# Seven products in the last feed-forward stage, rows to tokens by SP's queue, sides of x from scaled tiles

## The chip, the cores and the metric

The kernel runs as one program on one core of one Trainium2 chip. The time is that of the device from start to end, in microseconds; the kernel before took 956.64 us, the median of three runs (956.61 to 957.17). Lower is better.

## The reference

Two decoder layers work on 256 tokens of 1024 features (x, kept in float32). Each layer has four sublayers that add to x: a feed-forward stage, a token mixer (layer 0: a short gated convolution beside sliding-window attention; layer 1: block attention), cross-attention to a memory of 256 rows, and a second feed-forward stage. A final normalization ends it. The change works inside the feed-forward stages:

```python
def rmsnorm(x, g):
    x32 = x.astype(jnp.float32)
    y = x32 * lax.rsqrt(jnp.mean(x32 * x32, axis=-1, keepdims=True) + EPS)
    return y.astype(x.dtype) * g

def swiglu(x, w_gate, w_up, w_down):
    return (jax.nn.silu(x @ w_gate) * (x @ w_up)) @ w_down

for l in range(DEPTH):
    x = x + 0.5 * swiglu(rmsnorm(x, ffn1_norm[l]), ffn1_w_gate[l], ffn1_w_up[l], ffn1_w_down[l])
    ...
    x = x + 0.5 * swiglu(rmsnorm(x, ffn2_norm[l]), ffn2_w_gate[l], ffn2_w_up[l], ffn2_w_down[l])
return rmsnorm(x, final_norm)
```

w_gate and w_up are 1024 x 2816, w_down is 2816 x 1024. There are four such stages: ffn1 of layer 0, ffn2 of layer 0, ffn1 of layer 1 and ffn2 of layer 1, which is the last work before the final normalization.

## The kernel before

**x and its splits.** x lies with its features on the 128 partitions: eight tiles `x[:, k]` of 128 features by 256 tokens. Every product keeps float32's accuracy by splitting both factors into a rounded high part and the rest: x·w is taken as high·high + high·low + low·high, three matmuls for one. The scale of a norm is a number per token and is multiplied in when a product leaves PSUM, so a stage's matmuls start on x times the norm's gain.

**The stream of weights.** All weights come in one stream (class `Stream`) in chunks of 16 tiles of 128 x 128, 1 MB each. SP issues the loads into four buffers `raw` (`_load_to`); a load waits until VectorE (DVE) and ScalarE (ACT) are done with the buffer's last content. A chunk is two blocks of eight tiles. For each block ACT writes the high part `whi` (L143) and DVE the low part `wlo` (L144), into five buffers each, so that the splits run up to four blocks ahead of TensorE (PE).

**The order of the work.** `Order` is a planner that emits the instructions: a list of fillers (pieces of matmuls, each with a planned cost) and tasks put in with `pe.after(delay, fn, cost)`, which are emitted when the planner's clock, in planned ns, has come to their time. Afterwards a scheduler may still move an instruction along its engine's queue, except one marked `keep_in_program_order`, which stays behind all that its engine had been given before.

**A feed-forward stage** (`ffn`). The hidden width of 2816 is worked through in five groups of four tiles (512 columns) and one of two. For a group, `rows_of` computes gate and then up with tokens on the partitions: per tile of x (eight), half of the tokens (two) and part of the split (three) a matmul of 128 x 512, so 2 · 8 · 2 · 3 = 96 matmuls for a group. They are emitted in pieces (`part`) of 12 matmuls, which use one block of weights. The product of silu(gate) and up is turned back to features on partitions by `turned_back`: two DVE transposes, a store to DRAM and four loads on POOL's queue, and 22 to 34 us later (planned) a split by ACT and DVE into `h`. When gate and up are done, the down products follow: `downs` with features on partitions, and in the last stage `down_tok` with tokens on partitions, since the result leaves in that order.

**Seven products for eight** (`seven`, SEVEN = 12: the fourth group). Two of the four stages, named in `AT` with their place in the stream, compute this one group by a scheme of the Strassen kind. The factors are cut in four: x by halves of the tokens and halves of the features, the weights by halves of the features and by gate | up. Eight products of quarters would be 96 matmuls; seven products of sums of quarters are 7 · 4 · 3 = 84. Each is a filler of 12 matmuls that uses two blocks. `PLACES` says between which pieces of the other groups they stand. The sums of weight quarters are made by DMA: `load_bases` and `add` issue seven transfers of 1 MB on POOL's queue, five of which add to a tile in place of overwriting it; two further chunks come through SP's stream. The sums of x's quarters, the "sides", are made by DVE and ACT: `side` and `side2`, four times each, one for each pair of feature tiles (k, k + 4).

**The last stage's other work.** `to_tokens` brings x into token order for the final sum: four DVE transposes, and for each of them eight stores of 32 KB (in rows of 32 numbers) on POOL's queue to a DRAM tile `tok`, then one load of 1 MB into `xtok` on the same queue. `gfin`, the final gain, is loaded by SP to all partitions. `evac_tok` adds the down products to `xtok`, multiplies by the gain and the norm's factor, and stores the output.

Of the kernel before, what the change touches and what calls it, by code (L numbers as in the profile page):

```python
# [15 lines left out]
F32 = mybir.dt.float32  # L16
F32R = mybir.dt.float32r
AF = mybir.ActivationFunctionType
ALU = mybir.AluOpType
# [4 lines left out]
P = 128  # L24
# [24 lines left out]
AT = {("ffn2", 0): 52, ("ffn1", 1): 88}  # L49
# [216 lines left out]
def build(nc, tc, ctx, a):  # L266
# [50 lines left out]
    def col(key, k):  # L317
        c = VCOL[key] + k
        return vecs[:, c:c + 1]
# [188 lines left out]
    def to_tokens(out):  # L508


        tok = dram.tile([S, D], F32, name="tok")
        to = tok.rearrange("(c i) (k p j) -> p k i c j", i=32, p=4, j=32)
        for k in range(0, KT, 2):
            t = act.tile([P, 2 * S], F32, name="q2", bufs=2)
            tc.keep_in_program_order(nc.vector.transpose(t, x[:, k:k + 2].rearrange("p k s -> p (k s)")))
            for p in range(4):
                for i in range(2):
                    tc.keep_in_program_order(nc.gpsimd.dma_start(
                        to[p, k + i], t[32 * p:32 * p + 32, i * S:(i + 1) * S].rearrange("i (c j) -> i c j", j=32)))
        nc.gpsimd.dma_start(out, tok.rearrange("(u q) f -> q u f", u=2))  # L520
# [20 lines left out]
    def ffn(which, layer, n, nxt, first=False, last=False):  # L541
# [5 lines left out]
        def turned_back(f0, s, c):  # L547

            t = act.tile([P, 8 * c * 32], F32, name=("v", "kT" if sevens and f0 != SEVEN else "k2")[f0 // 4 % 2], bufs=1)
# [73 lines left out]
        def seven(f0, at):  # L623
# [26 lines left out]
            def part_of(p):  # L650
                return [(x[:, k, :P], x[:, k, P:], col(n.key, k)) for k in (p, p + 4)]

            def parted(t, at):
                hl = act.tile([P, 512], F32R, name="h", bufs=FT)
                hi, lo = hl[:, :S], hl[:, S:]
                nc.scalar.activation(hi, t, AF.Copy)
                nc.vector.tensor_tensor(lo, t, hi.bitcast(F32), op=ALU.subtract)
                for i in range(2):
                    sides[at[0], at[1] + i] = [m[:, i * P:(i + 1) * P] for m in (hi, lo)]

            def side(p):
                t, y = w2(), w1()[:, :P]
                s3, s1 = (t[:, i * P:(i + 1) * P] for i in range(2))
                (k0, k1, g), (q0, q1, gq) = part_of(p)
                tc.keep_in_program_order(nc.vector.tensor_scalar(y, k1, g, None, op0=ALU.mult))
                nc.vector.scalar_tensor_tensor(s3, k0, g, y, op0=ALU.mult, op1=ALU.subtract)
                nc.vector.scalar_tensor_tensor(s1, q1, gq, y, op0=ALU.mult, op1=ALU.subtract)
                parted(t[:, :S], (p, 0))

            def side2(p):  # L670
                t = w2()
                s2, s4 = (t[:, i * P:(i + 1) * P] for i in range(2))
                (k0, k1, g), (q0, q1, gq) = part_of(p)
                tc.keep_in_program_order(nc.vector.tensor_scalar(s2, k1, g, None, op0=ALU.mult))
                nc.vector.scalar_tensor_tensor(s2, k0, g, s2, op0=ALU.mult, op1=ALU.subtract)
                nc.vector.scalar_tensor_tensor(s2, q1, gq, s2, op0=ALU.mult, op1=ALU.add)
                nc.vector.scalar_tensor_tensor(s4, q0, gq, s2, op0=ALU.mult, op1=ALU.subtract)
                parted(t[:, :S], (p, 2))

            for p in range(4):  # L680
                pe.after(8000+3900*p, lambda p=p: side(p), 0)
                pe.after(32000+3900*p, lambda p=p: side2(p), 0)
# [101 lines left out]
        def down_tok():  # L784
# [30 lines left out]
            def evac_tok(u, at, ps):  # L815
                y = xtok[:, u, at]
                nc.vector.scalar_tensor_tensor(y, ps, 0.5, y, op0=ALU.mult, op1=ALU.add)
# [4 lines left out]
                if at.stop < D:  # L822
                    nc.gpsimd.tensor_tensor(y, y, gfin[:, at], op=ALU.mult)
                    return
                r = act.tile([P, 1], F32, name="rcol", bufs=2)
                nc.gpsimd.tensor_tensor(r, ms, mhalf[:, 0:1], op=ALU.pow)
                nc.vector.tensor_tensor(y, y, gfin[:, at], op=ALU.mult)
# [17 lines left out]
        if last:  # L845
            xtok = act.tile([P, 2, D], F32, name="bias", bufs=1)
            gfin = act.tile([P, D], F32, name="kT", bufs=1)
            src = a["final_norm"]
            nc.sync.dma_start(gfin, bass.AP(tensor=src.tensor, offset=src.offset, ap=[[0, P], [1, D]]))
            when_scaled(n, lambda: pe.after(6000, lambda: to_tokens(xtok), 0))  # L850
# [3 lines left out]
        if at is not None:  # L854
            if (which, layer) == ("ffn2", 0):
                load_bases(which, layer, False)
                pe.after(114000, lambda: load_bases("ffn1", 1, True), 0)
            assert ws.taken == FIRST + at * CHUNK, (ws.taken, at)
            for i, f in enumerate(seven(SEVEN, at)):
                ups.insert(PLACES[i] + i, f)  # L860
# [593 lines left out]
```

## Time and profile before

The profiled execution took 956.96 us; its trace spans 955.0 us. The other 1.96 us lie around the span.

| | |
|---|---|
| median of three runs | 956.64 us |
| profiled execution / its span | 956.96 / 955.0 us |
| PE busy | 947.9 us, 99% of the span |
| DVE / ACT / POOL busy | 75% / 60% / 13% |
| DMA | 230.20 MB, mean 241 GB/s |
| granted TensorE clock, mean | 0.998 |

How to read it: an engine's busy share is that over the whole program; what one stage can gain is read from the stage itself. A row of the timeline gives the start in us from the span's start, the duration, the engine, the line of the kernel, the operation, what it writes and reads, and in brackets how long its engine had been idle before and what ended that. A row of the waits gives who waited for whom, the total in us, the count and the longest. A row of the windows gives the stretch, each engine's busy us and instructions, the granted clock, the mean busy share of the 16 DMA engines and GB/s. A row of the groups ends in the total and the mean of one in ns. In the trace a tile stands under the name of its buffer's first letters (`q` for the transposed tile of `to_tokens`, `bias` for `xtok`, `k` and `bias` for the sums of weights, `w` for the scratch of the sides).

### The profile page before, as it was taken

What the parts mean: (1) busy time and instruction counts of PE and PEld (TensorE: products, weight loads), DVE (VectorE), ACT (ScalarE), POOL (GpSimd) and SP (SyncE); (2) the same over time, 40 slices, a digit from 0 to 9 for tenths busy, and PEclk for the clock granted to TensorE, in tenths of its full rate; (3) what the DMA queues carried; (4) which work ended last, traced back from release to release, by engine and by line L of the source; (5) the groups of instructions that cost most, each with busy time, mean ns of one, the idle gap of its engine ahead of it and who ended that gap; (6) DMA issues with size and microseconds to landing.
All of it is one profiled execution on the core that took longest, in us unless ns stands there. A gap on an engine that the chain in (4) does not pass through costs nothing.

```text
span 955.0 us, 15188 instructions
## 1 busy us (share of the span) xinstructions
PE 947.9 (99%) x5808; PEld 869.8 (91%) x5808; DVE 720.6 (75%) x1176; ACT 577.2 (60%) x938; POOL 128.8 (13%) x229
## 2 busy tenths in 40 slices
PE   9999999999999999999999999999999999999997
PEld 8888899999999888889988888999999998888896
DVE  7667667798878897976778797687877787577663
ACT  7555555697657766655557665456785675455541
POOL 0412120001000111121001111100000006411211
PEclk9999999999999999999999999999999999999999
DMA  9999976455536899889768978955645248897831
GB/s 371 310 372 308 327 238 216 173 188 190 187 132 243 231 276 336 255 283 358 240 178 263 339 240 272 309 205 179 246 148 187 103 176 291 308 282 239 268 132 44
DMA packets 38904, 230.20 MB, mean 241 GB/s; under 512 B 5928, under 2 KB 6952, under 8 KB 14896
## 3 DMA queue, kind: packets, MB, share of 16 engines
q1 hardware_dynamic: 26496, 183.48, 53.7%
q0 software_dynamic: 11760, 45.13, 17.5%
q8 instruction: 45, 0.74, 0.3%
q10 hardware_dynamic: 576, 0.64, 0.2%
q14 instruction: 27, 0.22, 0.1%
HBM read 215.56 MB, written 16.80 MB: 243 GB/s over the span
## 4 chain that ended last, share of the span: by engine, by line
PE 99%; DVE 0%; POOLq 0%; DVEq 0%; issue 0%
PE acc L582 12%; PE acc L583 12%; PE acc L584 12%; PE acc L418 8%; PE acc L423 7%; PE acc L425 7%; PE acc L424 7%; PE acc L419 4%; PE sc L418 3%; PE sc L582 2%; PE sc L584 2%; PE sc L583 2%; PE acc L808 2%; PE sc L419 2%; PE acc L806 2%; PE acc L807 2%
## 5 line engine op out<-in xcount | busy, mean ns | idle before, releaser
L144 DVE TENSOR_TENSOR wlo<-raw,whi 128x1024 fp32r<-128x1024 f32 (+2 forms) x367 | 415.8, 1141 | 163.2 <-ACT whi L143 160.6
L143 ACT ACTIVATE whi<-raw 128x1024 fp32r<-128x1024 f32 (+2 forms) x367 | 359.0, 987 | 264.4 <-PE acc L584 101.6
L583 PE MATMUL acc<-wlo,x 128*128 128x512 f32 x544 | 206.4, 379 | 0.0
L584 PE MATMUL acc<-whi,x 128*128 128x512 f32 x544 | 205.9, 379 | 0.0
L582 PE MATMUL acc<-whi,x 128*128 128x512 f32 x544 | 202.8, 381 | 0.0
L583 PEld LDWEIGHTS acc<-wlo,x 128*128 128x128 f32 x544 | 102.9, 189 | 15.3 <-DVE wlo L144 0.9
L582 PEld LDWEIGHTS acc<-whi,x 128*128 128x128 f32 x544 | 103.0, 189 | 14.7 <-ACT whi L143 0.3
L584 PEld LDWEIGHTS acc<-whi,x 128*128 128x128 f32 x544 | 102.9, 189 | 14.4
L418 PE MATMUL acc<-h,whi 128*128 128x512 f32 x330 | 108.5, 382 | 0.0
L419 PE MATMUL acc<-h,wlo 128*128 128x256 f32 x330 | 90.0, 273 | 0.0
L425 PE MATMUL acc<-h,wlo 128*128 128x256 f32 x322 | 87.7, 275 | 0.0
L424 PE MATMUL acc<-h,whi 128*128 128x256 f32 x322 | 87.7, 275 | 0.0
L423 PE MATMUL acc<-h,whi 128*128 128x256 f32 x322 | 86.5, 277 | 0.0
L425 PE MATMUL acc<-x,wlo 128*128 128x256 f32 x304 | 84.1, 278 | 0.0
L424 PE MATMUL acc<-x,whi 128*128 128x256 f32 x304 | 83.8, 277 | 0.0
L423 PE MATMUL acc<-x,whi 128*128 128x256 f32 x304 | 83.3, 278 | 0.0
L418 PEld LDWEIGHTS acc<-h,whi 128*128 128x128 f32 x330 | 62.4, 189 | 8.7
L419 PEld LDWEIGHTS acc<-h,wlo 128*128 128x128 f32 x330 | 63.3, 192 | 0.2
L424 PEld LDWEIGHTS acc<-h,whi 128*128 128x128 f32 x322 | 61.7, 192 | 0.1
L425 PEld LDWEIGHTS acc<-h,wlo 128*128 128x128 f32 x322 | 61.7, 192 | 0.1
L423 PEld LDWEIGHTS acc<-h,whi 128*128 128x128 f32 x322 | 60.6, 192 | 0.4 <-DVE x L486 0.2
L424 PEld LDWEIGHTS acc<-x,whi 128*128 128x128 f32 x304 | 58.2, 192 | 0.2
(277 smaller groups left out, 1682.4 us busy)
## 6 DMA issues: line engine op xcount, KB each, us to landing
raw<-in_w SPq DMA_DIRECT2D x167, 1024.0 KB, 6.4
bias<-in_w POOLq DMA_DIRECT2D x8, 1024.0 KB, 13.0
turn<-v POOLq DMA_DIRECT2D x12, 512.0 KB, 3.9
v<-turn POOLq DMA_DIRECT2D x48, 128.0 KB, 7.0
k<-in_w POOLq DMA_DIRECT2D x6, 1024.0 KB, 9.7
dists<-line POOLq DMA_DIRECT2D x2, 1536.0 KB, 12.7
turn<-k POOLq DMA_DIRECT2D x6, 512.0 KB, 8.9
raw<-in_memT SPq DMA_DIRECT2D x3, 1024.0 KB, 4.8
```

What stands on the lines that cost most here:

```text
L143: for ins in (self.nc.scalar.activation(hi[:, at], src, AF.Copy), self.nc.vector.tensor_tensor(lo[:, at], src, hi[:, at].bitcast(F32), op= ...
L144: self.nc.vector.tensor_tensor(lo[:, at], src, hi[:, at].bitcast(F32), op=ALU.subtract)):
L418: nc.tensor.matmul(ps, w[0], x2.both, start=start, stop=False)
L419: nc.tensor.matmul(ps[:, :S], w[1], x2.high, start=False, stop=stop)
L423: nc.tensor.matmul(ps[:, :S], w[0], x2.high, start=start, stop=False)
L424: nc.tensor.matmul(ps[:, :S], w[0], x2.low, start=False, stop=False)
L425: nc.tensor.matmul(ps[:, :S], w[1], x2.high, start=False, stop=stop)
L582: nc.tensor.matmul(ps[u], xh, wh, start=k == 0, stop=False)
L583: nc.tensor.matmul(ps[u], xh, wl, start=False, stop=False)
L584: nc.tensor.matmul(ps[u], xl, wh, start=False, stop=k == KT - 1)
L806: nc.tensor.matmul(ps, hh, wh, start=f == 0, stop=False)
L807: nc.tensor.matmul(ps, hh, wl, start=False, stop=False)
```

## The change

- The last stage (ffn2 of layer 1) gets an entry in `AT`: its fourth group is made by seven products as in the two others, with its own base loads (`load_bases`) at the stage's start.
- `to_tokens` is cut into four parts, emitted at 16, 25, 34 and 43 us of the planner's clock, each with one transpose on DVE and its eight stores, which SP's queue issues now in place of POOL's. The load of `xtok` (`from_tokens`) stays on POOL's queue and is emitted at 88 us; its buffer `bias` holds a sum of weights before that.
- `gfin` becomes two tiles of 512 columns in buffers of the name `p2`, loaded at 90 us; before it took `kT` from the stage's start.
- `turned_back` takes its buffers in another order where a stage has seven products: v, kT, v, k2, kT, v for the six groups (before: v, kT, v, k2, v, kT). In the last stage, which had v and k2 by turns, kT comes in.
- The sides, in all three stages: `scaled` writes x times the gain once, eight ACT operations into four tiles `p2`; then each of the four sides is made for all four pairs at once, by two DVE operations on 256 columns, and split by one ACT and one DVE operation on 512 columns. Before, each pair had seven DVE operations on 128 columns, and two ACT and two DVE operations on 256 columns.

```diff
-AT = {("ffn2", 0): 52, ("ffn1", 1): 88}
+AT = {("ffn2", 0): 52, ("ffn1", 1): 88, ("ffn2", 1): 144}
...
-    def to_tokens(out):
-        tok = dram.tile([S, D], F32, name="tok")
+    def to_tokens(tok, k):
         to = tok.rearrange("(c i) (k p j) -> p k i c j", i=32, p=4, j=32)
-        for k in range(0, KT, 2):
-            t = act.tile([P, 2 * S], F32, name="q2", bufs=2)
-            tc.keep_in_program_order(nc.vector.transpose(t, x[:, k:k + 2].rearrange("p k s -> p (k s)")))
-            for p in range(4):
-                for i in range(2):
-                    tc.keep_in_program_order(nc.gpsimd.dma_start(
-                        to[p, k + i], t[32 * p:32 * p + 32, i * S:(i + 1) * S].rearrange("i (c j) -> i c j", j=32)))
-        nc.gpsimd.dma_start(out, tok.rearrange("(u q) f -> q u f", u=2))
+        t = act.tile([P, 2 * S], F32, name="q2", bufs=2)
+        tc.keep_in_program_order(nc.vector.transpose(t, x[:, k:k + 2].rearrange("p k s -> p (k s)")))
+        for p in range(4):
+            for i in range(2):
+                tc.keep_in_program_order(nc.sync.dma_start(
+                    to[p, k + i], t[32 * p:32 * p + 32, i * S:(i + 1) * S].rearrange("i (c j) -> i c j", j=32)))
...
-            t = act.tile([P, 8 * c * 32], F32, name=("v", "kT" if sevens and f0 != SEVEN else "k2")[f0 // 4 % 2], bufs=1)
+            t = act.tile([P, 8 * c * 32], F32, name=(("v", "kT", "v", "k2", "kT", "v") if sevens else ("v", "k2") * 3)[f0 // 4], bufs=1)
...
-            for p in range(4):
-                pe.after(8000+3900*p, lambda p=p: side(p), 0)
-                pe.after(32000+3900*p, lambda p=p: side2(p), 0)
+            def scaled():
+                for k in range(KT):
+                    if k % 2 == 0:
+                        sides["x", k // 2] = xg = act.tile([P, 2, S], F32, name="p2", bufs=4)
+                    tc.keep_in_program_order(nc.scalar.activation(xg[:, k % 2], x[:, k], AF.Copy, scale=col(n.key, k)))
+            def side(i):
+                sides["t", i] = t = w2()
+                for j in range(2):
+                    at = slice(2 * j, 2 * j + 2)
+                    k0, k1, q0, q1 = (sides["x", j + 2 * q][:, :, u * P:(u + 1) * P] for q in range(2) for u in range(2))
+                    ahead = sides["t", 2 * (i - 2)].rearrange("p (k s) -> p k s", k=4)[:, at] if i > 1 else None
+                    x0, x1, op = ((k0, k1, ALU.subtract), (q1, k1, ALU.subtract),
+                                  (q1, ahead, ALU.add), (q0, ahead, ALU.subtract))[i]
+                    out = t.rearrange("p (k s) -> p k s", k=4)[:, at]
+                    tc.keep_in_program_order(nc.vector.tensor_tensor(out, x0, x1, op=op))
+                hi, lo = (act.tile([P, 512], F32R, name="h", bufs=FT) for _ in range(2))
+                nc.scalar.activation(hi, t, AF.Copy)
+                nc.vector.tensor_tensor(lo, t, hi.bitcast(F32), op=ALU.subtract)
...
+            pe.after(6000, scaled, 0)
+            for i, d in enumerate((10000, 15000, 20000, 25000)):
+                pe.after(d, lambda i=i: side(i), 0)
...
-            xtok = act.tile([P, 2, D], F32, name="bias", bufs=1)
-            gfin = act.tile([P, D], F32, name="kT", bufs=1)
-            src = a["final_norm"]
-            nc.sync.dma_start(gfin, bass.AP(tensor=src.tensor, offset=src.offset, ap=[[0, P], [1, D]]))
-            when_scaled(n, lambda: pe.after(6000, lambda: to_tokens(xtok), 0))
+            tok, back = dram.tile([S, D], F32, name="tok"), {}
+            def from_tokens():
+                back["x"] = t = act.tile([P, 2, D], F32, name="bias", bufs=1)
+                tc.keep_in_program_order(nc.gpsimd.dma_start(t, tok.rearrange("(u q) f -> q u f", u=2)))
+            def last_factors():
+                gfin.extend(act.tile([P, 512], F32, name="p2", bufs=4) for _ in range(2))
+                src = a["final_norm"]
+                for i, g in enumerate(gfin):
+                    nc.sync.dma_start(g, bass.AP(tensor=src.tensor, offset=src.offset + i * 512, ap=[[0, P], [1, 512]]))
+            pe.after(90000, last_factors, 0)
+            for k in range(0, KT, 2):
+                pe.after(16000 + 9000 * (k // 2), lambda k=k: to_tokens(tok, k), 0)
+            pe.after(88000, from_tokens, 0)
...
-            if (which, layer) == ("ffn2", 0):
+            if which == "ffn2":
                 load_bases(which, layer, False)
+            if not layer:
                 pe.after(114000, lambda: load_bases("ffn1", 1, True), 0)
```

More of the change, by code (lines that the diff above doesn't have):

```diff
@@ L648, in seven @@
             sides = {}
[L650 to L655, printed above, removed]
+            def scaled():
[3 more added lines that the diff above has]
+                    tc.keep_in_program_order(nc.scalar.activation(xg[:, k % 2], x[:, k], AF.Copy, scale=col(n.key, k)))
@@ L656, in parted @@
                 nc.scalar.activation(hi, t, AF.Copy)
                 nc.vector.tensor_tensor(lo, t, hi.bitcast(F32), op=ALU.subtract)
[L658 to L678, printed above, removed]
@@ L680, in seven @@
-            for p in range(4):
-                pe.after(8000+3900*p, lambda p=p: side(p), 0)
-                pe.after(32000+3900*p, lambda p=p: side2(p), 0)
+                for p in range(4):
+                    sides[p, i] = [m[:, p * P:(p + 1) * P] for m in (hi, lo)]
+            pe.after(6000, scaled, 0)
+            for i, d in enumerate((10000, 15000, 20000, 25000)):
+                pe.after(d, lambda i=i: side(i), 0)
             kept = {}
@@ L815, in evac_tok @@
             def evac_tok(u, at, ps):
+                xtok = back["x"]
                 y = xtok[:, u, at]
+                g = gfin[at.start // 512][:, at.start % 512:at.start % 512 + at.stop - at.start]
                 nc.vector.scalar_tensor_tensor(y, ps, 0.5, y, op0=ALU.mult, op1=ALU.add)
@@ L822, in evac_tok @@
                 if at.stop < D:
-                    nc.gpsimd.tensor_tensor(y, y, gfin[:, at], op=ALU.mult)
+                    nc.gpsimd.tensor_tensor(y, y, g, op=ALU.mult)
                     return
@@ L826, in evac_tok @@
                 nc.gpsimd.tensor_tensor(r, ms, mhalf[:, 0:1], op=ALU.pow)
-                nc.vector.tensor_tensor(y, y, gfin[:, at], op=ALU.mult)
+                nc.vector.tensor_tensor(y, y, g, op=ALU.mult)
                 out = a["out"][u * P:(u + 1) * P]
@@ L845, in ffn @@
         if last:
-            xtok = act.tile([P, 2, D], F32, name="bias", bufs=1)
-            gfin = act.tile([P, D], F32, name="kT", bufs=1)
-            src = a["final_norm"]
-            nc.sync.dma_start(gfin, bass.AP(tensor=src.tensor, offset=src.offset, ap=[[0, P], [1, D]]))
-            when_scaled(n, lambda: pe.after(6000, lambda: to_tokens(xtok), 0))
+            gfin = []
+            tok, back = dram.tile([S, D], F32, name="tok"), {}
[11 more added lines that the diff above has]
+            pe.after(88000, from_tokens, 0)
         at = AT.get((which, layer))
```

## The prediction

> **What bounds the kernel now.** I read the page first: the span, the engines' shares and the chain that ended last.
>
> ```profile
> span 955.0 us, 15188 instructions
> PE 947.9 (99%) x5808; PEld 869.8 (91%) x5808; DVE 720.6 (75%) x1176; ACT 577.2 (60%) x938; POOL 128.8 (13%) x229
> PE 99%; DVE 0%; POOLq 0%; DVEq 0%; issue 0%
> ```
>
> PE is busy for 947.9 of 955.0 us, and 99% of the chain is matmul after matmul. So time is saved only where PE gets fewer matmuls, and lost only where PE has to wait. The next question is what a stage with seven products takes and whether PE waits in it; two stages of the kernel before have them already. Their borders, from PE's timeline (gate and up begin with L582; the down products begin with L418, in the last stage with L806):
>
> ```profile
> 310.45 0.38 PE L582 MATMUL acc<-whi,x 128*128 128x512 f32 x1
> 422.27 0.38 PE L418 MATMUL acc<-h,whi 128*128 128x512 f32 x1
> 480.08 0.38 PE L582 MATMUL acc<-whi,x 128*128 128x512 f32 x1
> 591.67 0.38 PE L418 MATMUL acc<-h,whi 128*128 128x512 f32 x1
> 776.91 0.38 PE L582 MATMUL acc<-whi,x 128*128 128x512 f32 x1
> 777.13 0.38 PE L583 MATMUL acc<-wlo,x 128*128 128x512 f32 x1
> 891.10 0.38 PE L806 MATMUL acc<-whi,h 128*128 128x512 f32 x1
> ```
>
> The same stretches in the view by windows (us; then busy us of PE, PEld, DVE, ACT and POOL; clock, DMA share, GB/s):
>
> ```profile
> 310.45:422.27 111.82, 111.82 (x520) 97.55 (x519) 94.22 (x138) 69.99 (x93) 17.69 (x27) 1.00 0.92 280
> 480.08:591.67 111.59, 111.59 (x521) 97.70 (x519) 90.49 (x133) 67.53 (x91) 15.90 (x26) 1.00 0.84 264
> 776.91:891.10 114.19, 114.19 (x533) 99.97 (x531) 80.09 (x98) 62.27 (x80) 34.46 (x59) 1.00 0.82 272
> ```
>
> Gate and up take 111.82 us in ffn2 of layer 0 and 111.59 in ffn1 of layer 1, with seven products, and 114.19 in the last stage, without. The clock is full in all three.
>
> **The change, part by part.**
>
> *The matmuls.* 96 become 84, 12 fewer. One takes 0.22 us from start to start (776.91, 777.13); the exact figure is 114.19 us over 528 matmuls and the two turns of the norm, 0.216. 12 · 0.216 = 2.59 us less. The stages say the same: 114.19 − 111.59 = 2.60. I take −2.59.
>
> *A wait at the first product.* ffn2 of layer 0 is 0.23 us longer than ffn1 of layer 1. PE's waits and DVE's timeline there:
>
> ```profile
> PEld tr L700 <- DVE wlo L144: 0.3, 1, 0.3
> PEld acc L583 <- DVE wlo L144: 0.2, 1, 0.2
> 321.24 0.42 DVE L383 TENSOR_REDUCE ms<-tr 128x2 f32<-128x256 f32 x1 [3.23 <-PE tr L379]
> 321.77 1.22 DVE L144 TENSOR_TENSOR wlo<-k,whi 128x1024 fp32r<-128x1024 f32 x1
> ```
>
> The fifth filler of the stage is the first product and uses two blocks in 2.6 us. DVE stands 3.23 us in its queue before L383, which waits for PE's transposes of the norm's sums; behind it stands the `wlo` of the product's second block, which comes late. The last stage also follows a memory sublayer, and its row is alike:
>
> ```profile
> 787.91 0.42 DVE L383 TENSOR_REDUCE ms<-tr 128x2 f32<-128x256 f32 x1 [3.44 <-PE tr L379]
> ```
>
> Today ordinary pieces follow there and hide it. With the product in that place I expect the other stage's 0.23 us, +0.23; the bounds are 0 (as in ffn1 of layer 1) and 0.5 (the two waits' sum, by their rounded rows).
>
> *The sides.* In ffn2 of layer 0, by groups:
>
> ```profile
> L657 DVE TENSOR_TENSOR h<-w,h 128x256 fp32r<-128x256 f32 x8 | 3.2, 414 | 0.0
> L656 ACT ACTIVATE h<-w 128x256 fp32r<-128x256 f32 x8 | 3.2, 409 | 2.0 <-DVE w L667 2.0
> L343 ACT ACTIVATE x<-x,vecs 128x256 fp32r<-128x256 f32 x3 | 1.5, 495 | 0.0
> L358 DVE TENSOR_TENSOR w<-w,w 128x512 f32<-128x512 f32 x2 | 1.4, 684 | 0.0
> L666 DVE SCALAR_TENSOR_TENSOR w<-x,vecs,w 128x128 f32<-128x128 f32 x4 | 1.4, 340 | 0.0
> L665 DVE TENSOR_SCALAR w<-x,vecs 128x128 f32<-128x128 f32 x4 | 1.1, 276 | 0.0
> L720 ACT ACTIVATE h<-tr 128x512 f32<-128x512 f32 x1 | 0.6, 597 | 0.2 <-PE tr L701 0.2
> ```
>
> DVE before: 8 · 0.276 + 20 · 0.340 + 8 · 0.414 = 12.3 us. After: 8 operations on 256 columns like L657 and 4 on 512 like L358, 8 · 0.414 + 4 · 0.684 = 6.0. ACT before: 8 · 0.409 = 3.3; after: 8 · 0.495 + 4 · 0.597 = 6.3. So DVE gains 6 us a stage and ACT pays 3. Neither is on the path: 0 us. The cover on ACT is its idle time, 70 us busy of 112; the eight scaling operations come at the third filler, 4 us in one piece, while the blocks of the first product are already split. Without that cover the next block's `whi` would be up to 4 us late, against a lead of about 3. In the last stage DVE would have 94.2 − 6.3 + four transposes of 0.7 = 90.7 us in 111.6, as much as ffn1 of layer 1 has, whose PE does not wait.
>
> *The weights' sums.* The seven transfers of 1 MB, their adds and the extra splits are those of ffn2 of layer 0: same neighbour before, same places. They are within its 111.82 us, so nothing is added for them. POOL, which issues them, loses the 32 stores.
>
> *The stores on SP's queue.* This is what neither older stage has. The rows of today's stores, on POOL's queue (the 9 us hold one batch of eight; then issues, KB, us to landing), and SP's issue of a weight load:
>
> ```profile
> q0 software_dynamic: 298, 0.33, 13.5%
> tok<-q POOLq DMA_DIRECT2D x8, 32.0 KB, 5.3
> L518 POOL DMA_DIRECT2D tok<-q x32 | 18.5, 584 | 9.6 <-DVE q L515 4.8 <-DMA tok<-q 4.6
> L117 SPq DMA_DIRECT2D raw<-in_w x167: 327/328/328, 7.2 to 916.9; - x167
> ```
>
> In the 9 us from 814 to 823 POOL's queue moved 0.33 MB, the batch's 0.26 and some of another, in 13.5% of the 16 engines' time: 1.2 us at most for a batch, about 1.0 by its part of the bytes. SP's issuing would take 8 · 0.33 = 2.6 us a batch; POOL's took 0.584 each, 4.7 us. SP spends nearly all its time waiting for buffers, so the issuing itself is free unless a weight load that is urgent stands behind it. The batch waits for its transpose on DVE, and so could hold the load behind it; but those loads wait for `wlo` on the same engine, so SP's order follows DVE's. Price: 0.
>
> When would a load be urgent? ffn2 of layer 0 again, DMA by windows of 10 us, and its worst moment on ACT, DVE and PE:
>
> ```profile
> 340.00:350.00 10.00, 10.00 (x48) 8.74 (x48) 8.60 (x11) 7.12 (x10) 4.62 (x7) 1.00 0.88 280
> 350.00:360.00 10.00, 10.00 (x48) 8.77 (x47) 10.00 (x20) 7.00 (x10) 0.00 (x0) 1.00 1.03 263
> 370.00:380.00 10.00, 10.00 (x48) 8.74 (x48) 7.67 (x10) 8.30 (x12) 0.42 (x1) 1.00 1.01 387
> 369.83 2.00 ACT L143 ACTIVATE whi<-raw 128x1024 fp32r<-128x1024 f32 x2 [1.79 <-DMA raw<-in_w]
> 370.92 1.23 DVE L144 TENSOR_TENSOR wlo<-raw,whi 128x1024 fp32r<-128x1024 f32 x1 [3.12 <-ACT whi L143]
> 375.65 0.38 PE L582 MATMUL acc<-whi,x 128*128 128x512 f32 x1
> ```
>
> From about 40 to 70 us into the stage the DMA engines are full (share 1.0), because the adds run beside the weights. At 369.83 ACT had waited 1.79 us for a weight load. The `wlo` made of it ends at 370.92 + 1.23 = 372.15; it is the 31st block of the stage, and PE comes to it with the 26th filler at 375.65 (25 fillers of 2.59 us after 310.45, and half a us of turns and waits). So 3.5 us of lead are left where it is thinnest. The four batches are emitted after the fillers that pass 16, 25, 34 and 43 us, behind the splits then already in DVE's queue: about 23, 31, 37 and 46 us into the stage. The last two fall into or just before the full stretch, and their transfers delay the weights by 2 · 1.0 to 2 · 1.2 = 2.0 to 2.4 us. That is less than 3.5: 0 us, with a lead of about 1.1 to 1.5 left. This is the thinnest cover in the sum. If it is gone, each further us of delay is a us of PE.
>
> The Trainium skill, "DMA: Bandwidth & Descriptors", section "Queues, rings and completion order", speaks against the move: an engine takes turns between the queues that have work for it, packet by packet, so that on POOL's queue the stores share with the weights, while on SP's own they stand whole in front of them. By that rule the weights wait for the full 2.4 us and not for a part, which is what the sum assumes.
>
> *The rest.* `xtok`'s load is emitted at 88 us and the gain's at 90 us, some 23 us before the stage's end; the first use follows half of the down products later (its row today, and the load's us to landing):
>
> ```profile
> 919.43 0.68 DVE L817 SCALAR_TENSOR_TENSOR bias<-acc,bias 128x512 f32<-128x512 f32 x1
> bias<-tok POOLq DMA_DIRECT2D x1, 1024.0 KB, 13.0
> ```
>
> That is 919.4 − 776.9 = 142 us into the stage, so the cover is some 40 us after a landing in 13: 0. The order of `turned_back`'s buffers: no row shows a wait for them: 0. The program's end after the last matmul keeps its operations: 0.
>
> *The sum.* 956.96 − 2.59 + 0.23 = 954.60 for the profiled execution. That one is 0.32 us above the median of the runs; from the median, 956.64 − 2.36 = **954.3 us**.
>
> **The rivals.** A measurement of this kernel can tell about 0.2%, 1.9 us, from no change: under 954.7 counts as faster, over 958.6 as slower.
>
> *A, the wait at the first product goes.* DVE's lighter sides and another order of its queue let the block come in time in ffn2 of layer 0 and in the last stage: 956.64 − 2.59 − 0.23 = 953.8. For it: ffn1 of layer 1 has no such wait. Against it: DVE waits there for PE, not for its own work.
>
> *B, SP's issuing counts in the full stretch.* The weights stand still for the 16 issues of the last two batches, 16 · 0.33 = 5.3 us, against 3.5 of lead: 1.8 us of waiting, 954.3 + 1.8 = 956.1, no difference that can be told. For it: the loads of that stretch land just in time. Against it: several loads are on their way then (ACT's wait ended with one that others followed), so an issue that is late by 2.6 us finds a queue that is not empty.
>
> *C, slower: a store of short rows costs SP's queue as much as it cost POOL to issue.* A batch has 2048 rows of 128 bytes, and the trace shows no such rows on SP's queue. At 0.584 us a store two batches stop the weights for 16 · 0.584 = 9.3 us, less 3.5 of lead: 5.8 us, 954.3 + 5.8 = 960.1. It ends slower than before from 3.5 + 2.4 + 1.9 = 7.8 us for two batches, 0.49 us a store. Against it: POOL's queue moved the same rows at 0.13 to 0.15 us a store (1.0 to 1.2 us for eight). The Trainium skill, on the same page, section "Specifications", says that under 512 bytes an engine reads, modifies and writes; by that rule C gets its price, but the row of POOL's queue doesn't bear it out.
>
> *D, the seven products don't shorten the stage.* If the down products had to wait for `h`, the gain would come back there: 956.6. Against it: the two older stages have the same products and go from L584 to L418 at a matmul's usual pace, as the row before 422.27 shows:
>
> ```profile
> 422.06 0.38 PE L584 MATMUL acc<-whi,x 128*128 128x512 f32 x1
> ```
>
> **How the numbers follow.** Forecast (954.3, its own range 953.9 to 954.7) 0.58; A 0.11; B, with all of its smaller sizes, 0.19; C 0.09; D 0.03. The range of 8 in 10 goes from A, 953.6 with 0.2 of spread, to the upper end of B, 956.6. Faster: the forecast and A, less a little of its upper edge, 0.68; same: B, D and that edge, 0.23; slower: C, 0.09.
>
> **What would show it.** Right: gate and up of the last stage take 111.6 to 111.9 us, PE's waits there name `wlo` once, for 0.2 to 0.5 us, and the thinnest lead some 60 us into the stage is 1 us or more. B or C: PE waits for `wlo` 50 to 80 us into the stage, ACT waits for `raw` longer than 1.8 us before it, and the stores' rows on SP show 0.33 us (B) or far more to landing than 5.3 (C). A: no wait on `wlo` in ffn2 of layer 0. The sides: DVE's busy time falls by some 6 us in ffn2 of layer 0 and in ffn1 of layer 1, ACT's rises by 3. The prediction is wrong if PE waits in the last stage for more than 1 us, or if the older two stages get longer.

## The result, and the profile after

The changed kernel takes 963.22 us, the median of four runs (961.48 to 963.72), against 956.62 us for the kernel before on the same chip: a ratio of 1.0064, with a 95% interval of 1.0047 to 1.0082. It is slower, where the forecast was 954.3 us with a range up to 956.6. The profiled execution took 963.72 us, 6.76 us more than that of before and 9.1 us more than the 954.60 that the sum gave for it.

From the page of the changed kernel: span, engines, DMA queues (packets, MB, share of 16 engines) and the chain that ended last:

```profile
span 961.9 us, 15192 instructions
PE 948.4 (99%) x5796; PEld 868.7 (90%) x5796; DVE 726.5 (76%) x1153; ACT 594.1 (62%) x968; POOL 116.1 (12%) x204
...
q1 hardware_dynamic: 35056, 182.43, 52.2%
q0 software_dynamic: 11744, 51.42, 20.5%
...
PE 94%; DMA 3%; DVE 2%; issue 0%; ACT 0%; POOLq 0%; DVEq 0%; ACTq 0%; SPq 0%
```

The 12 matmuls are gone (5808 to 5796), but the chain, which was 99% PE, now passes through DMA and DVE. The stages show where. The view by windows of the changed kernel (us; busy us of PE, PEld, DVE, ACT, POOL; clock, DMA share, GB/s): gate and up of ffn2 of layer 0, of ffn1 of layer 1 and of the last stage, and then the last one cut at PE's long wait:

```profile
310.34:422.16 111.82, 111.82 (x521) 97.55 (x519) 90.26 (x115) 72.82 (x99) 17.77 (x27) 1.00 0.93 284
479.96:591.55 111.59, 111.59 (x520) 97.70 (x519) 85.65 (x107) 69.21 (x91) 15.93 (x26) 1.00 0.84 268
776.80:897.36 120.56, 114.92 (x520) 99.19 (x519) 92.61 (x119) 72.74 (x99) 18.44 (x28) 0.97 0.91 276
...
836.97:842.15 5.18, 0.01 (x2) 0.01 (x1) 0.02 (x1) 1.11 (x2) 0.00 (x0) 0.91 1.00 307
842.15:848.00 5.85, 5.38 (x12) 3.97 (x13) 5.85 (x8) 5.50 (x9) 0.57 (x1) 0.50 0.81 197
848.00:897.36 49.36, 49.36 (x230) 43.22 (x229) 39.59 (x51) 27.44 (x36) 9.04 (x16) 1.00 0.89 307
```

The two older stages take what they took. The last one takes 120.56 us, 8.74 more than the 111.82 that the forecast gives it. For 5.18 us PE stands still, and for the next 5.85 us it runs at a clock of 0.50. In PE's timeline it is 11.55 us from the start of the matmul at 836.60 to that of the thirteenth after it, at 848.15; at the usual pace thirteen take 13 · 0.216 = 2.81. The difference is the whole 8.74: about 5.3 for the long wait, 0.8 for a second, short one, and 2.6 for the half clock.

Who waited for whom in the last stage (total, times, longest):

```profile
ACT whi L143 <- DMA raw<-in_w: 13.3, 1, 13.3
...
PE acc L579 <- ACT whi L143: 5.2, 1, 5.2
...
PE acc L580 <- DVE wlo L144: 0.5, 1, 0.5
...
PEld tr L689 <- DVE wlo L144: 0.3, 1, 0.3
```

And the chain of waits in order of time, around 820 us (start, duration, step):

```profile
815.22 5.78 DMA tok<-q
821.09 19.85 DMA raw<-in_w
841.04 1.06 ACT whi L143
842.13 1.24 DVE wlo L144
843.40 0.79 PE acc L580
```

The chain runs from the third batch of stores into a weight load that was issued at 821.09 and landed 19.85 us later. SP's own timeline, and a summary of its stores (min/median/max ns of one issue, then us to landing), show both sides of it:

```profile
805.91 1.60 SPq L117 DMA_DIRECT2D raw<-in_w  x2
807.78 6.85 SPq L516 DMA_DIRECT2D tok<-q  x8
814.73 0.40 SPq L117 DMA_DIRECT2D raw<-in_w  x1
815.22 5.76 SPq L516 DMA_DIRECT2D tok<-q  x8
821.09 1.30 SPq L117 DMA_DIRECT2D raw<-in_w  x2
822.77 20.94 SPq L516 DMA_DIRECT2D tok<-q  x8
843.81 0.87 SPq L117 DMA_DIRECT2D raw<-in_w  x2
...
L516 SPq DMA_DIRECT2D tok<-q x32: 302/457/9546, 798.9 to 843.4; - x32
...
DMA to landing us min/median/max: 1.7/6.4/20.9
```

First, the loads issued at 821 stood behind the third batch's rows, of which the last landed at 833.6. Second, the fourth batch held SP for 20.94 us (one store alone 9.5 us), so that no load was issued between 822.4 and 843.8.

Why the rows took so long is seen in the DMA queues of the stretch from 824 to 832 us (packets, MB, share of 16 engines), the changed kernel first, then the one without stores (the first experiment):

```profile
q0 software_dynamic: 221, 1.64, 98.5%
q1 hardware_dynamic: 206, 0.03, 4.0%
```

```profile
q0 software_dynamic: 156, 1.11, 66.5%
q1 hardware_dynamic: 157, 1.16, 35.8%
...
raw<-in_w SPq DMA_DIRECT2D x2, 1024.0 KB, 19.7
```

In both, SP's queue (q1) gets about one packet for one of POOL's (q0). Without stores SP's packets are weights of 8 KB, 1.16 MB in 8 us. With them its packets are rows of 128 bytes: 206 packets carry 0.03 MB, and the weights behind them stand still. The last line is a caution: without stores, too, the loads issued in this stretch took 19.7 us to land (median of two) beside the adding transfers. So the 19.85 us are not by themselves the mark of the rows. What differs is how many loads are on their way: by 821 us eight loads of the stage had been issued without stores and six in the changed kernel, and until 843.8 only two more followed there. The trace's packets, counted by queue and size in pieces of 2 us (those of 4 bytes and of 4 KB left out), show the rows in the changed kernel:

```
us         POOL's queue             SP's queue
822-824    50 of 8 KB, 647 ns       205 of 128 B
824-826    53 of 8 KB, 629 ns        24 of 128 B
826-828    49 of 8 KB, 628 ns        63 of 128 B
828-830    48 of 8 KB, 632 ns        47 of 128 B
830-832    50 of 8 KB, 628 ns        71 of 128 B
832-834    19 of 8 KB, 628 ns        58 of 128 B, 71 of 8 KB (309 ns)
...
842-844    none                    1711 of 128 B (13 ns), 9 of 8 KB
```

The rows' own transfer is short where nothing else runs: 13 ns a packet, 2048 · 13 / 16 = 1.7 us a batch. Beside an adding transfer each waits for a packet of 628 ns: from 824 to 834 us 263 rows passed, and 263 · 0.628 / 16 = 10.3 us, which is that stretch.

On the queues, the Trainium skill ("DMA: Bandwidth & Descriptors", section "Queues, rings and completion order") says that an engine goes round the queues that have work, a packet from each. The 221 and 206 packets agree. For the clock, the Trainium skill ("TensorE: Matmul & The Clock Gate", section "What's actually happening") names half rate after an idle window of about 3.4 us; the wait of 5.18 us and a clock of 0.50 for 6.8 us, from 841.2 to 848.0, agree. Shorter waits in other runs were followed by half clock too (last section), so 3.4 us of waiting is not needed here.

### The profile page after: what moved, and what is told of

Its sections match the earlier page's. It is cut to its first block, busy times and chain, and to the rows that moved or that the text cites. A ratio compares the mean times of both kernels' runs of the same rounds, so it can differ in the third digit from the quotient of the medians.

```text
span 961.9 us, 15192 instructions
## 1 busy us (share of the span) xinstructions
PE 948.4 (99%) x5796; PEld 868.7 (90%) x5796; DVE 726.5 (76%) x1153; ACT 594.1 (62%) x968; POOL 116.1 (12%) x204
## 3 DMA queue, kind: packets, MB, share of 16 engines
q1 hardware_dynamic: 35056, 182.43, 52.2%
q0 software_dynamic: 11744, 51.42, 20.5%
## 4 chain that ended last, share of the span: by engine, by line
PE 94%; DMA 3%; DVE 2%; issue 0%; ACT 0%; POOLq 0%; DVEq 0%; ACTq 0%; SPq 0%
PE acc L580 11%; PE acc L581 11%; PE acc L579 11%; PE acc L418 8%; PE acc L423 7%; PE acc L425 7%; PE acc L424 7%; PE acc L419 4%; PE sc L418 3%; DMA raw<-in_w 2%; PE tr L689 2%; PE tr L688 2%; PE tr L690 2%; PE acc L797 2%; PE acc L796 1%; PE sc L419 1%
## 5 line engine op out<-in xcount | busy, mean ns | idle before, releaser
L144 DVE TENSOR_TENSOR wlo<-raw,whi 128x1024 fp32r<-128x1024 f32 (+2 forms) x363 | 409.6, 1140 | 154.6 <-ACT whi L143 152.2
L143 ACT ACTIVATE whi<-raw 128x1024 fp32r<-128x1024 f32 (+2 forms) x363 | 353.7, 986 | 244.7 <-PE acc L581 82.7
L580 PE MATMUL acc<-wlo,x 128*128 128x512 f32 x528 | 201.7, 382 | 0.6 <-DVE wlo L144 0.5
L579 PE MATMUL acc<-whi,x 128*128 128x512 f32 x528 | 196.5, 382 | 5.2 <-ACT whi L143 5.2
L581 PE MATMUL acc<-whi,x 128*128 128x512 f32 x528 | 200.7, 381 | 0.0
L579 PEld LDWEIGHTS acc<-whi,x 128*128 128x128 f32 x528 | 100.4, 190 | 20.1 <-ACT whi L143 5.9
L580 PEld LDWEIGHTS acc<-wlo,x 128*128 128x128 f32 x528 | 100.3, 190 | 16.6 <-DVE wlo L144 2.4
L581 PEld LDWEIGHTS acc<-whi,x 128*128 128x128 f32 x528 | 100.4, 190 | 14.1
```

The costliest lines, as they stand in the source:

```text
L143: for ins in (self.nc.scalar.activation(hi[:, at], src, AF.Copy), self.nc.vector.tensor_tensor(lo[:, at], src, hi[:, at].bitcast(F32), op= ...
L144: self.nc.vector.tensor_tensor(lo[:, at], src, hi[:, at].bitcast(F32), op=ALU.subtract)):
L579: nc.tensor.matmul(ps[u], xh, wh, start=k == 0, stop=False)
L580: nc.tensor.matmul(ps[u], xh, wl, start=False, stop=False)
L581: nc.tensor.matmul(ps[u], xl, wh, start=False, stop=k == KT - 1)
```

## The experiments

Each is the changed kernel with the edit shown. Its runs stand beside runs of the kernel before on the same chip (medians 956.62 to 956.71 us). "Gate and up" is that of the last stage in the profiled execution, 120.56 us in the changed kernel.

**1. No stores at all.**

```diff
-        for p in range(4):
-            for i in range(2):
-                tc.keep_in_program_order(nc.sync.dma_start(
-                    to[p, k + i], t[32 * p:32 * p + 32, i * S:(i + 1) * S].rearrange("i (c j) -> i c j", j=32)))
...
-                tc.keep_in_program_order(nc.gpsimd.dma_start(t, tok.rearrange("(u q) f -> q u f", u=2)))
+                tc.keep_in_program_order(nc.gpsimd.dma_start(t.rearrange("p u f -> p (u f)"), a["xT"].rearrange("p k s -> p (k s)")))
```

> Leaves out the 32 stores to tok (the four transposes stay); xtok is loaded from x as it lies in DRAM, so the final sum is made of wrong tokens. Turns theory (in the changed kernel a store's 128-byte rows on SP's queue each take a turn against an 8 KB add on POOL's queue, and the weight loads stand behind them): without the stores PE does not wait in the last stage, gate and up take 111.6 to 111.9 us, the time is 954.0 to 954.6. Products theory (the third set of seven products, or the sides made from scaled tiles, make PE wait by themselves): still 961 to 964, with ACT waiting some 13 us for raw.

Measured: 955.31 us (954.49 to 958.67), ratio 0.9991 [0.9981, 1.0000]. The windows of gate and up and of the down products:

```profile
776.60:888.42 111.82, 111.82 (x521) 97.54 (x519) 93.31 (x122) 73.19 (x101) 18.20 (x28) 1.00 0.93 290
888.42:945.78 57.36, 57.36 (x331) 52.05 (x329) 34.77 (x45) 22.41 (x28) 10.57 (x13) 1.00 0.44 155
```

PE does not wait. In gate and up the seven products, the wait at the first of them and the sides come out as forecast, so the loss there needs the stores. The median is 1.0 us above the forecast, and above the range expected for this run: three of the ten runs took over 956 us, for which no cause was found.

**2. The stores on POOL's queue, at the changed kernel's times.**

```diff
-                tc.keep_in_program_order(nc.sync.dma_start(
+                tc.keep_in_program_order(nc.gpsimd.dma_start(
```

> The changed kernel with the 32 stores at the same times, but issued on POOL's queue as before the change. Turns theory: stores and adds share one queue there, so the weights keep their turn on SP's queue; no wait of PE beyond 0.5 us, 954.0 to 955.0; the adds may land some us later. Bytes theory (the stage simply moves too much while the adds run): the same bytes, so still 960 to 964.

Measured: 965.72 us (961.68 to 968.87), ratio 1.0092 [1.0058, 1.0126]; gate and up 118.09 in the profiled execution, the fastest of the four. The expectation missed: leaving SP's queue does not help. POOL also issues the adding transfers, in order, and these stood behind the stores. Rows of POOL's timeline, then of the waits:

```profile
830.02 0.59 POOL L516 DMA_DIRECT2D tok<-q  x1 [8.02 <-DMA bias<-in_w]
...
836.74 0.93 POOL L633 DMA_DIRECT2D k<-in_w  x1 [0.43 <-ACT h L561]
...
850.35 0.97 POOL L633 DMA_DIRECT2D bias<-in_w  x1
```

```profile
ACT whi L143 <- DMA bias<-in_w: 6.0, 1, 6.0
```

In the changed kernel those two adds were issued at 819.49 and 828.69. Packets say how differently the queues carry the same 8192 rows: this kernel's page has 26352 packets on SP's queue and 12768 on POOL's, so the stores are 35056 − 26352 = 8704 packets on SP's queue and 12768 − 11744 = 1024 on POOL's. Both counts hold 512 packets of 4 bytes. The rest, by size, is 8192 packets of 128 bytes on SP's queue and 512 of 2 KB on POOL's, so that there 16 rows share a packet.

**3. The stores on SP's queue, after the adds, 5 us apart.**

```diff
-                pe.after(16000 + 9000 * (k // 2), lambda k=k: to_tokens(tok, k), 0)
+                pe.after(64000 + 5000 * (k // 2), lambda k=k: to_tokens(tok, k), 0)
```

> The changed kernel with the four batches of stores on SP's queue emitted at 64, 69, 74 and 79 us of the planner's clock in place of 16, 25, 34 and 43, when the adds on POOL's queue (which ended 64.6 us into the stage) are over. Turns theory: no 8 KB adds to take turns with, so 954.0 to 955.0. Order theory (the stores hold SP's queue whatever runs beside them, by their issue and their rows): each batch still holds the weights by 4 us or more; 956 to 962, with PE waiting 65 to 90 us into the stage.

Measured: 962.49 us (959.61 to 963.24), ratio 1.0050 [1.0033, 1.0068]; gate and up 113.95, and the down products 63.55 in place of 57.36. Turns beside adds alone, as I then held, do not explain it. SP's timeline:

```profile
837.01 0.33 SPq L117 DMA_DIRECT2D raw<-in_w  x1
842.60 10.35 SPq L516 DMA_DIRECT2D tok<-q  x8
...
860.73 9.80 SPq L516 DMA_DIRECT2D tok<-q  x16
870.63 0.87 SPq L117 DMA_DIRECT2D raw<-in_w  x2
```

Here the order on SP costs: between the load at 837.01 and that at 870.63 SP issued four batches, the last two back to back, and only two loads (at 853.06 and 860.24). The last add was issued at 831.22 and landed at 845.8, so only the first batch met it. The loss moves to the down products' start, with 6.8 us at half clock from 900.9.

**4. No third set of products; the stores on SP's queue and the new sides stay.**

```diff
-AT = {("ffn2", 0): 52, ("ffn1", 1): 88, ("ffn2", 1): 144}
+AT = {("ffn2", 0): 52, ("ffn1", 1): 88}
```

> The changed kernel without the third set of seven products: eight quarters' work in the last stage as before the change, so no adds there, but the stores on SP's queue at 16, 25, 34 and 43 us and the new sides in the two older stages. Turns theory: no adds in the last stage, so the weights are at most 2 us later and PE does not wait: 956.4 to 957.2, as before the change. Order theory: SP is held as in the changed kernel, PE waits some us in the last stage, 959 to 965. If the new sides cost anything, it shows here in the two older stages.

Measured: 956.81 us (956.40 to 957.25), ratio 0.9998 [0.9988, 1.0007]; gate and up 114.18, as before, and no wait of PE. The window, the stores' summary, and two of their rows in SP's timeline:

```profile
777.27:891.45 114.18, 114.18 (x532) 99.97 (x531) 80.12 (x98) 62.34 (x80) 16.09 (x27) 1.00 0.83 272
```

```profile
L516 SPq DMA_DIRECT2D tok<-q x32: 302/465/1894, 796.6 to 832.3; - x32
...
804.90 9.81 SPq L516 DMA_DIRECT2D tok<-q  x8
...
823.14 9.51 SPq L516 DMA_DIRECT2D tok<-q  x8
```

A store holds SP as long as in the changed kernel in the median (465 ns against 457), but none for 9.5 us. Two of the batches still hold SP for 9.8 and 9.5 us with no add beside them, and PE does not wait. In this stage each block of weights serves 12 matmuls, where a product of the seven uses two blocks for 12, so a load may come later here. The stores without the third set, and the sides, cost nothing.

**5. One store of 256 KB a batch, in rows of 2 KB.**

```diff
-        to = tok.rearrange("(c i) (k p j) -> p k i c j", i=32, p=4, j=32)
+        to = tok.rearrange("(p u) (h f) -> h u p f", u=2, h=2)
...
+        tc.keep_in_program_order(nc.sync.dma_start(to[k // 4, k // 2 % 2], t))
```

> The changed kernel, but each batch is one store of 256 KB in rows of 2 KB on SP's queue, at the same four times and in the same place among the loads; the order of tokens and features in tok is left out, so the final sum is made of wrong numbers. Rows theory (it is the 2048 rows of 128 bytes a batch that hold SP's issue and take turns against the adds' 8 KB): 128 rows a batch, no wait of PE beyond 0.5 us, gate and up 111.8 to 112.5 us, 954.9 to 956. Bytes theory (what the stage moves is too much while the adds run): the same bytes, so 960 to 964.

Measured: 956.47 us (954.84 to 957.75), ratio 0.9996 [0.9987, 1.0006]; gate and up 111.81, the down products 57.91. The same bytes at the same times on the same queue, in 1/16 of the rows and 1/8 of the issues, cost gate and up nothing. It changes both the number of rows and the time on SP, and so doesn't tell the two apart.

**6. The adding transfers of the last stage left out.**

```diff
-                tc.keep_in_program_order(nc.gpsimd.dma_start(t, w, accum_op=ALU.add))
+                if (which, layer) != ("ffn2", 1):
+                    tc.keep_in_program_order(nc.gpsimd.dma_start(t, w, accum_op=ALU.add))
```

> The changed kernel without the five adding transfers of the last stage (the two base loads stay, so five of the seven products take wrong sums of weights). The stores stay on SP's queue at 16, 25, 34 and 43 us. If the weights stand still because the stores' rows take turns with the adds: no such wait, 955 to 956. If the stores hold SP's queue alone, whatever runs beside them, and the seven products' faster use of weights is what makes it felt: still 959 to 964, PE waiting 50 to 70 us into the stage.

Measured: 954.66 us (954.28 to 956.88), ratio 0.9984 [0.9974, 0.9993]; gate and up 111.82. SP's timeline:

```profile
798.89 4.49 SPq L516 DMA_DIRECT2D tok<-q  x8
...
822.80 4.99 SPq L516 DMA_DIRECT2D tok<-q  x8
```

Nothing else is taken out, and the time is near the forecast's 954.3. A batch now holds SP for 4.5 to 5.0 us, 0.56 to 0.62 a store, where it held it for 5.8 to 20.9 us in the changed kernel. Experiments 4 and 6 together: at these four times, rows on SP's queue cost nothing without the adds. Experiment 3 shows that at other times they can.

**7. The stores on POOL's queue, early (12, 15, 18 and 21 us).**

```diff
+                tc.keep_in_program_order(nc.gpsimd.dma_start(
...
+                pe.after(12000 + 3000 * (k // 2), lambda k=k: to_tokens(tok, k), 0)
```

> The changed kernel with the stores on POOL's queue, emitted at 12, 15, 18 and 21 us. With the stores on POOL's queue at 16 to 43 us, PE waited because two adds were issued behind them too late. Queue theory (either queue can bear the stores if nothing urgent stands behind them): three batches and the first of the adds no longer collide, the adds of the weights come at most some 4 us later than in ffn2 of layer 0, gate and up take 111.8 to 114 us, 955 to 957.5. If the stores disturb by their bytes or rows wherever they are: 960 to 966.

Measured: 958.95 us (957.12 to 962.13), ratio 1.0023 [1.0013, 1.0032]; gate and up 112.81, the down products 60.38. Better than experiment 2, and outside both ranges expected: gate and up are within the first, but an added block still came late (ACT waited 8.2 us for one), and then a turned group.

**8. The stores on SP's queue after the adds, 9 us apart.**

```diff
+                pe.after(66000 + 9000 * (k // 2), lambda k=k: to_tokens(tok, k), 0)
+            pe.after(102000, from_tokens, 0)
```

> The changed kernel with the stores on SP's queue at 66, 75, 84 and 93 us, 9 us apart and behind the adds, the load of xtok at 102 us. With 64 to 79 us, 5 us apart, two batches stood in a row on SP's queue and a load behind them came some 10 us late. Queue theory: one batch at a time costs the weights 2 to 4 us of a lead of 6 to 7: PE waits 0.5 us at most, 954.9 to 956.5. If SP's queue is held by any batch for as long as in the changed kernel (up to 20 us): 958 to 964.

Measured: 955.68 us (954.57 to 959.77), ratio 0.9992 [0.9981, 1.0003]; gate and up 111.81, the down products 57.38. Spread out and behind the adds, the same 32 stores cost gate and up nothing in the profiled execution (954.61 us), though a batch held SP for up to 9.25 us.

**9. Only the last two batches after the adds** (the first two at 16 and 25 us, as in the changed kernel).

```diff
+                pe.after((16000, 25000, 84000, 93000)[k // 2], lambda k=k: to_tokens(tok, k), 0)
+            pe.after(102000, from_tokens, 0)
```

> The first two batches stay at 16 and 25 us on SP's queue, the last two go to 84 and 93 us, behind the adds (xtok's load at 102 us, as in the kernel with all four spread). Theory (rows of 128 bytes take turns with the adds, and only the last two batches meet them): gate and up of the last stage take 111.8 to 112.2 us, no wait for raw or whi of over 1 us, the clock stays full; 954.3 to 955.7 us. Rival (every batch costs, because SP's rows put all later loads behind by some us, and the first two only use up the lead): PE waits 1 to 4 us there, stage 113 to 117 us, 956.5 to 960.

Measured: 962.26 us, in two groups: five runs at 955.19 to 957.61, seven at 961.06 to 965.76; ratio 1.0040 [1.0017, 1.0063]. Gate and up take 111.82 us, as the theory has it, but the time doesn't come out, and the rival's wait in gate and up isn't there either. In the profiled execution (963.47) the loss is in the down products, 65.47 us, where a turned group came late. The window, and the wait:

```profile
889.00:954.47 65.47, 61.00 (x330) 53.84 (x329) 35.50 (x48) 23.53 (x32) 11.30 (x14) 0.95 0.49 166
```

```profile
ACT h L561 <- DMA k<-turn: 9.8, 1, 9.8
```

**10. Only the first two batches after the adds** (the last two at 34 and 43 us).

```diff
+                pe.after((84000, 93000, 34000, 43000)[k // 2], lambda k=k: to_tokens(tok, k), 0)
+            pe.after(102000, from_tokens, 0)
```

> The other way round: the first two batches go to 84 and 93 us, the last two stay at 34 and 43 us. Theory: the stretch with the adds holds the same two batches as in the changed kernel; ACT waits over 5 us for a weight load, PE waits 2 to 6 us, and the clock falls to 0.5 after it; stage 115 to 121 us, 957 to 963. Rival (all four are needed for the loss): the lead that the first two no longer take is enough; stage 111.8 to 112.5 us, 954.3 to 956.

Measured: 964.20 us (958.11 to 968.40), ratio 1.0069 [1.0045, 1.0094]; gate and up 114.42, the down products 67.95. SP's timeline again:

```profile
822.17 18.90 SPq L516 DMA_DIRECT2D tok<-q  x8
841.18 4.64 SPq L117 DMA_DIRECT2D raw<-in_w  x4
```

In gate and up two batches are enough for a loss: the one that meets the adds holds SP for 18.90 us, and no load is issued until 841.18. PE's wait there, 1.8 us, is shorter than the 2 to 6 that I expected, and the clock stays full there. Most of the loss, some 10 us, comes at the down products, as in experiment 9 with the other two batches early. So the times of 9 and 10 do not tell which batches matter; only their gate and up do (111.82 and 114.42).

**11. All four batches before the adds.**

```diff
+                pe.after(5000 + 6000 * (k // 2), lambda k=k: to_tokens(tok, k), 0)
```

> All four batches on SP's queue before the adds: emitted after the fillers that pass 5, 11, 17 and 23 us (16, 25, 34 and 43 in the changed kernel). Theory (128-byte rows on SP's queue lose only while adds are on POOL's): the batches land before 819 us, no weight load takes over 15 us to land, PE waits under 0.5 us in gate and up, 111.8 to 112.2 us there, 954.3 to 956 us. Rival (the four batches' 6 to 7 us of transfer, wherever they lie ahead of the adds, leave the weights too little lead): ACT waits over 5 us for a weight or an added block between 820 and 860 us, PE over 1 us, 957 to 963 us.

Measured: 965.37 us (962.75 to 968.76), ratio 1.0093 [1.0078, 1.0109]; gate and up 118.88. The theory missed and the rival holds. SP's timeline, and the wait:

```profile
798.66 7.47 SPq L516 DMA_DIRECT2D tok<-q  x8
...
810.67 0.38 SPq L117 DMA_DIRECT2D raw<-in_w  x1
...
812.37 9.49 SPq L516 DMA_DIRECT2D tok<-q  x8
821.96 3.47 SPq L117 DMA_DIRECT2D raw<-in_w  x4
```

```profile
ACT whi L143 <- DMA raw<-in_w: 17.8, 5, 6.5
```

By 821 us SP had issued five loads of the stage here, six in the changed kernel, and eight in experiments 1 and 8. The four issued from 821.96 to 825.10 stood beside the adds and took 8.1, 15.0, 21.9 and 26.7 us to land. So the rows need not meet the adds: it is enough that they hold loads back until the adds have begun.

**12. Experiment 8 with the load of `xtok` at 110 us** (the edit is shown against experiment 8).

```diff
-            pe.after(102000, from_tokens, 0)
+            pe.after(110000, from_tokens, 0)
```

> The kernel with the four batches at 66, 75, 84 and 93 us once more, with xtok's load of 1 MB at 110 us in place of 102, out of the way of the last two turned groups. Theory: gate and up 111.8, down products 57.4 us; the runs near 957 of the other kernel come from the down products' start, where the load stood beside the turned groups; so fewer of them: median 954.5 to 955.2. Rival (those runs have another cause): as the other kernel, 955.0 to 956.5; if the load lands too late, DVE waits for it at 920 us and the time is over 957.

Measured: 955.89 us (954.61 to 956.67), ratio 0.9989 [0.9980, 0.9997]. The theory on `xtok` missed: runs over 956 remain. The profiled execution (956.54) is one of them:

```profile
888.58:947.59 59.01, 57.90 (x331) 51.84 (x329) 35.60 (x48) 23.64 (x32) 11.30 (x14) 1.00 0.52 180
```

Gate and up took 111.82; the 1.65 us are lost at the down products, where ACT waited 9.1 us for a turned group (`k`). This and experiment 8 are the best versions with all the work in it, about 0.1% ahead of the kernel before. That is less than the 0.2% that the prediction takes as the least that can be told, and the interval of experiment 8 includes no change.

## Why the prediction was wrong, step by step

*What bounds the kernel, the matmuls, the wait at the first product*: right. Gate and up take 111.82 us in every run in which PE does not wait (1, 6, 8, 12), the −2.59 and +0.23 of the sum.

*The sides*: right that they cost nothing (the older stages still take 111.82 and 111.59 us). The sizes were smaller than forecast: DVE's busy time fell by 4.0 us in ffn2 of layer 0 and 4.8 in ffn1 of layer 1, not 6; ACT's rose by 2.8 and 1.7, not 3.

*The weights' sums, xtok, the gain, the buffers' order*: "nothing is added" held for gate and up when nothing else was in the way. For the down products' start it held only in part: experiment 12 loses 1.65 us there with gate and up undisturbed. The gain was not loaded at 90 us either: SP issued its two loads at 796.2, 19 us into the stage, ahead of the first batch.

*The stores on SP's queue*: this is the step that failed, and the prediction had named it "the thinnest cover in the sum". It priced two batches by their transfer, 2.0 to 2.4 us against 3.5 us of lead. The transfer is of that order (1.7 us a batch alone, by its packets, where the prediction has 1.0 to 1.2). What stands in the weights' way is longer, for two reasons that the runs show. One is turns: the price of a row on SP's queue is not its bytes but a turn, and beside the adds a turn costs a packet of 628 ns. The prediction quoted the rule of turns, and read it as the batch's whole transfer in front of the weights; the count of the rows that meet the adds, times the other queue's packet, was the sum to make. The other is order: "the issuing itself is free" at 0.33 us a store, from a weight load. It was 0.56 to 0.62 in experiment 6, 0.63 to 1.23 in experiment 4 and 0.7 to 2.6 in the changed kernel (5.8 to 20.9 us for eight). While SP stands there it issues no load. That alone is no loss (4, 6 and 8): it becomes one where the loads held back come too late for PE. How much of the 8.74 us each of the two makes alone was not separated: experiment 5 takes both away, and 3 and 11 show the order at work where hardly a row meets the adds.

*A cost with no term*: the clock. A wait of 5.18 us was followed by 6.8 us at half clock, and so cost half as much again (some 2.6 us). The prediction had put each us of delay beyond the lead at one us of PE.

*The program's end*: put at 0. From the last matmul's start to the end of the span it takes 0.69 us more than before, in the changed kernel and in experiments 1, 8 and 12 alike. So the forecast's 954.60 is met in experiment 8 (954.61) partly by luck: its last stage begins 0.45 us earlier than before.

*The rivals.* A fell: ffn2 of layer 0 still takes 111.82 us, with its wait. D fell. B named the right place (no load issued behind the last two batches) with a price five times too small: 5.3 us, where they held SP for 5.76 + 20.94 = 26.7 us. C, at a chance of 0.09, had the direction and nearly the size (960.1 against 963.2); its price of 0.584 us a store is what experiment 6 measures. But that price alone decides nothing, for experiments 4 and 6 pay it and lose nothing. It decides where the loads held back then stand beside the adds (the changed kernel, 10 and 11) or where batches follow each other closely (3), and no rival said so.

*What would show it* worked in the main: PE waited 60 to 65 us into the stage, and ACT before it for `raw`, with stores that took up to 20.9 us to land. The long wait was for `whi`, not for `wlo` as named.

**Still open.** Why the kernels with the third set differ from run to run (experiment 9 by 10 us, the kernel before by up to 3). The waits seen lie at the adds and at the down products' first group, but there is one trace of each kernel, so what changes between runs is not shown. Open too is how the 8.74 us divide between turns and order.

## What to carry to other kernels

A transfer moved to another queue is priced there by its packets, and by what the other queues hold at that moment: count the rows that are still to move then, multiply by the packet beside them, divide by the 16 engines, and set that against the lead of whatever stands behind. With all 2048 rows of a batch that is a bound, 2048 · 0.628 / 16 = 80 us; in the changed kernel 263 rows met the adds after 824 us, which makes 10. Moving it also moves its place in an engine's order of issue, so ask of both engines what is then issued later (SP's weights, POOL's adds). When a wait is possible at all, add what the clock takes after it.

## What was not expected of the hardware

- The same 8192 rows of 128 bytes make 8192 packets on SP's queue and 512 of 2 KB on POOL's, beside 512 of 4 bytes on either.
- A single store's issue held SP for 9.5 us (302 to 9546 ns, by the traffic), where a weight load's took 0.33 in the kernel before.
- An adding transfer's packet of 8 KB takes 628 ns, a weight load's mostly 309 (324 beside the adds from 834 to 840 us).
- Half clock also follows shorter waits: in experiment 2 a wait of 2.0 us (to 867.2) was followed by 3.4 us at half clock from 868.5, and in experiment 11 two of 0.9 and 0.8 us (to 846.1 and 847.3) by 3.4 us from 848.5, where two of 0.6 and 0.8 us some 7 us before had none. In experiment 10 a wait of 3.1 us (to 927.4) had none.
- From the last matmul's start to the end of the span it is 7.19 us in the changed kernel and 6.50 before. The closing drain of POOL takes 4.99 us in place of 4.13; without the third set (experiment 4) it is 4.42. The reason stays open.
